# Gate and up with four paired slabs in a row: the residual kept in DRAM, its tiles used for summed weights, and a fifth weight place

## The chip, the cores and the metric

The kernel runs on one core of a Trainium2 chip. The metric is the device time of one execution in microseconds (us). The kernel computes everything in 32-bit floats; each factor of a product is split into a high part that TensorE multiplies exactly enough and a low part, and a product is made of three matmuls (high x high, high x low, low x high).

## The reference, cut to what matters

One encoder block over 256 rows of 2048 features: four mixers side by side, cross attention, and a gated MLP, each added to the residual `x`, then a last norm. The change lies in the MLP:

```python
def swiglu(h, w_gate_up, w_down):
    gate, up = jnp.split(h @ w_gate_up, 2, axis=-1)
    return (jax.nn.silu(gate) * up) @ w_down
...
        x = x + swiglu(rms_norm(x, norm_g[l, 2]), w_gate_up[l], w_down[l])
    return rms_norm(x, final_norm_g)
```

`w_gate_up` is 2048 x 11264, `w_down` is 5632 x 2048. The residual `x` isn't read between the norm ahead of `w_gate_up` and the sum behind `w_down`.

## The kernel before, in words

**Weights come as a stream.** All weights lie in DRAM as 296 slabs of 16 blocks of 128 x 128, 1 MB each, in the order of use. Class `Stream` loads a slab into one of three `raw` buffers (`_load`, L94, on the queue of SyncE, SP), and splits it in halves or phases: ScalarE (ACT) casts the piece to the high part `wh` (L135, L147), VectorE (DVE) subtracts it for the low part `wl` (L136, L148). A piece's `wh` and `wl` lie in a *place*. Three places come from the pool `wp`, a fourth from the pool `st.extra`, which takes every fourth piece (L90). `_fill` (L166) sees to it that three pieces beyond the one in use are begun, two where there is no `extra`. `take` (L177) and `take_sums` (L192) hand the pieces to TensorE (PE).

**Two kinds of slab.** In `paired_rows` (L463) a plan of letters says how each slab is used. An N slab is plain: 16 blocks, each row of four times two halves of the 256 rows, eight parts of three matmuls of 512 columns (L432 to L434), 24 matmuls. An S slab holds the blocks of two k tiles for two column blocks (gate and up) and is multiplied with the two halves of the rows as a 2 x 2 by 2 x 2 block product in seven products instead of eight, by sums of weight blocks and of activations: seven parts, 21 matmuls. Its pieces come in four phases (`_sums`, L140): two raw quarters, one raw quarter, two sums, two sums, that is 1024, 512, 1024 and 1024 columns. The sums of activations (`combine`, L437) are made once, in tiles `z`.

**Sums made by the transfer.** For S slabs of gate and up (`SUMMED`) the third phase's two sums are made by DMA: two loads of the last quarter into both halves of a tile `two` (L101, SP), and then a load of the middle quarters that adds onto it, issued by GpSimd (L102, POOL). This is requested at the load of the slab just before the S slab; there are two such tiles. `raw` then needs only three quarters (L105, 768 KB), and DVE makes two additions (L158) instead of four.

**Order of the MLP.** `gate_up` (L1047) first makes columns 0 to 511 of gate and up plainly (slabs 120 to 127, `gemm_rows`), and meanwhile the combinations of the first activations by a background generator. Then come ten groups (j = 1 to 10) of 8 slabs, each with the plan `GROUP = "NNSNSNSN"`, L45. When the last S slab of a group is through, `mixed` (L1064) adds up four of the eight PSUM banks, `gated` (L1073) makes the silu of gate, and at the group's end `upped` (L1079) multiplies and `store_turned` (L553) writes the result to DRAM. The banks of the paired sums and the others change their roles from group to group (`swap`). `fetch` (L1087) loads the results back as activations `f` of the down product and splits them: 22 of 44 during the groups, the others afterwards, since they lie in the tiles `z` and `h3` that the groups still use. `down` (L1138) makes two passes of 22 slabs with plans of their own; it adds to the residual, tiles `res`, when its sums are through. There the S slabs load the whole slab and DVE makes all four sums.

A background (class `Background`, L204) holds the generators; `poll` lets one go a step when the DVE work owed is small. The framework orders the instructions of an engine by its own priorities, the SP queue and POOL run ahead as far as buffers are free.

Of the kernel before, what the change touches and what calls it, by code (L numbers as in the profile page):

```python
# [23 lines left out]
P = 128  # L24
# [20 lines left out]
GROUP = "NNSNSNSN"  # L45
# [3 lines left out]

PAIRED = {a + i for a, plan in [(GATE_UP + 8 * j, GROUP) for j in range(10)] + [(DOWN, PASSES[0]), (DOWN + 22, PASSES[1])]  # L50
          for i, x in enumerate(plan) if x == "S"}
SUMMED = {i for i in PAIRED if i < DOWN}
# [201 lines left out]
class Block:  # L254
# [208 lines left out]
    def paired_rows(self, w, cols, slots, sums, plan, mixed, first, ready=None, late=0, before=None, swap=False):  # L463
# [23 lines left out]
        for i, kind in enumerate(plan):  # L487
            if before:
                before(i)
            if kind == "S":  # L490
# [76 lines left out]
    def run(self):  # L567
# [21 lines left out]
        self.gk = [nc.dram_tensor(f"state{i}", (R, P), F32, kind="Internal").ap() for i in range(4)]  # L589
        self.vd = nc.dram_tensor("values", (P, 8 * 512), F32, kind="Internal").ap()  # L590
# [18 lines left out]
        with self.tc.tile_pool(name="wx", bufs=1) as st.extra:  # L609
            self.attention(self.mixers())  # L610
# [256 lines left out]
    def attention(self, ps):  # L867
        tc, nc, act, st = self.tc, self.nc, self.act, self.st
        with tc.tile_pool(name="atp", bufs=1) as atp, tc.tile_pool(name="kp", bufs=1) as kp, \
# [111 lines left out]
            st.extra = None  # L981
# [65 lines left out]
    def gate_up(self, gp, f, z):  # L1047
# [77 lines left out]
        ps = self.gemm_rows("w_gate_up", [0, DFF], self.h3,  # L1125
                            parts=[(range(8), [0]), (range(8, 12), [0]), (range(12), [1]), (range(12, 16), [0]), (range(12, 16), [1])],
                            before=lambda n: n in (1, 3) and self.bg.drain(self.late if n == 1 else last))
# [3 lines left out]
        early = self.bg.add(fetch(0, FT - 22, 3, 2.0, 15))  # L1131
        self.bg.drain(comb)
        for j in range(1, DFF // 512):
            upped(j, self.paired_rows("w_gate_up", [j * 512, DFF + j * 512], self.h3, sums, GROUP, mixed, gated, swap=j % 2 == 0)[0])
        self.bg.drain(early)
        self.fetch = self.bg.add(fetch(FT - 22, FT, 6, SOON))

    def down(self, f, sp):  # L1138
# [54 lines left out]
        for i, plan in enumerate(PASSES):  # L1193
# [5 lines left out]
            def before(j):  # L1199
                while plan[j] == "S" and len(made) <= plan[:j].count("S"):  # L1200
                    self.bg.step(next(e for e in self.bg.q if e[0] is g))
                if late and j == len(plan) - 2:
                    st.extra = None
# [687 lines left out]
```

## Time and profile before

| what | us |
|---|---|
| runs shown, median of 3 | 1436.53 (1435.76 to 1437.61) |
| the profiled execution | 1434.72 |
| its span in the trace | 1432.9 |
| TensorE busy | 1423.0 |
| VectorE busy | 1145.7 |
| ScalarE busy | 815.8 |

The profiled execution's own time is 1.8 us longer than its span. Busy time of an engine is the union of its instructions. A window's line gives its length and then, engine by engine, busy time and number of instructions, the granted clock of TensorE as a share of full speed, the mean busy share of the 16 DMA engines and the GB/s that they moved. A grouped line gives busy time, mean ns of one instruction, idle time of the engine ahead of them and what ended it. Durations of neighbours on one engine overlap somewhat; the distance from start to start is the pitch. q1 is the DMA queue that SP issues on, q0 that of POOL.

### The profile page before, as it was taken

The page shows a single profiled execution, that of the slowest core. Times are in us where ns is not written, and L with a number is a line of the kernel's source. Part 1 is how long each engine was busy: PE and PEld are TensorE (multiplying, and loading weights), DVE is VectorE, ACT ScalarE, POOL GpSimd, SP SyncE. Part 2 cuts the span into 40 slices and gives each one's busy share as a digit, 9 for nine tenths or more (in the row PEclk, how much of TensorE's full clock was granted, in tenths as well). Part 3 has the DMA queues.
Part 4 walks back from the last instruction along what each step waited for, and adds up shares of the span by engine and source line. Part 5 has one row for each costly group of instructions (what it writes and reads, how often), then busy time and mean ns, then how long its engine had stood idle before and what let it go on. Part 6 is the DMA issues. An engine that isn't in the chain of part 4 may idle for free.

```text
span 1432.9 us, 18653 instructions
## 1 busy us (share of the span) xinstructions
PE 1423.0 (99%) x6589; PEld 1181.4 (82%) x6589; DVE 1145.7 (80%) x1738; ACT 815.8 (57%) x1183; POOL 234.6 (16%) x306
## 2 busy tenths in 40 slices
PE   9999999999999999999999999999999999999997
PEld 8888888888888888888888888888888888788886
DVE  6667868777877767777677888889888888989997
ACT  7556565446745555556455556555555556655655
POOL 0000100013212223531430121122011002000000
PEclk9999999999999999999999999999999999999999
DMA  9877554456667787865986989899999887665554
GB/s 350 299 291 247 205 202 166 171 172 224 198 199 232 235 271 246 275 201 171 287 242 207 283 280 289 275 275 285 294 293 289 264 265 227 217 231 180 193 219 147
DMA packets 73038, 343.80 MB, mean 240 GB/s; under 512 B 10957, under 2 KB 12654, under 8 KB 45168
## 3 DMA queue, kind: packets, MB, share of 16 engines
q1 hardware_dynamic: 54848, 288.98, 57.6%
q0 software_dynamic: 17664, 52.97, 15.6%
q8 instruction: 51, 0.84, 0.2%
q10 hardware_dynamic: 432, 0.66, 0.1%
q14 instruction: 43, 0.35, 0.1%
HBM read 322.12 MB, written 20.45 MB: 239 GB/s over the span
## 4 chain that ended last, share of the span: by engine, by line
PE 98%; DVE 1%; DMA 0%; ACT 0%; issue 0%; SPq 0%; ACTq 0%
PE pg L432 22%; PE pg L433 22%; PE pg L434 22%; PE pm L432 7%; PE pm L434 7%; PE pm L433 7%; PE pg L380 4%; PE pg L381 2%; PE pm L1344 1%; PE pm L1022 1%; PE pm L993 1%; PE pm L1753 0%; DMA raw<-in_W 0%; DVE res L282 0%; PE pm L994 0%; PE pm L1518 0%
## 5 line engine op out<-in xcount | busy, mean ns | idle before, releaser
L136 DVE TENSOR_TENSOR wl<-raw,wh 128x1024 fp32r<-128x1024 f32 (+1 forms) x413 | 494.1, 1211 | 167.6 <-ACT wh L135 164.8
L135 ACT CAST wh<-raw 128x1024 fp32r<-128x1024 f32 (+1 forms) x413 | 424.7, 1043 | 282.9 <-PE pg L434 188.3
L432 PE MATMUL pg<-wh,act 128*128 128x512 f32 (+1 forms) x1191 | 465.5, 391 | 0.0
L433 PE MATMUL pg<-wl,act 128*128 128x512 f32 (+1 forms) x1191 | 463.9, 389 | 0.1
L434 PE MATMUL pg<-wh,act 128*128 128x512 f32 (+1 forms) x1191 | 463.8, 390 | 0.0
L432 PEld LDWEIGHTS pg<-wh,act 128*128 128x128 f32 x1191 | 224.0, 188 | 47.9 <-issue 1.5
L434 PEld LDWEIGHTS pg<-wh,act 128*128 128x128 f32 x1191 | 223.9, 188 | 47.5 <-DVE act L282 0.6
L433 PEld LDWEIGHTS pg<-wl,act 128*128 128x128 f32 x1191 | 224.0, 188 | 46.5 <-DVE wl L136 1.2
L147 ACT CAST wh<-raw 128x1024 fp32r<-128x1024 f32 (+1 forms) x150 | 137.4, 921 | 149.6 <-PE pg L434 53.8
L148 DVE TENSOR_TENSOR wl<-raw,wh 128x1024 fp32r<-128x1024 f32 (+1 forms) x150 | 155.9, 1060 | 52.8 <-ACT wh L147 52.6
L433 PE MATMUL pm<-wl,act 128*128 128x512 f32 x309 | 120.3, 389 | 0.1
L432 PE MATMUL pm<-wh,act 128*128 128x512 f32 x309 | 120.2, 389 | 0.0
L434 PE MATMUL pm<-wh,act 128*128 128x512 f32 x309 | 120.2, 389 | 0.0
L380 PE MATMUL pg<-act,wh 128*128 128x512 f32 x256 | 90.5, 395 | 0.0
L381 PE MATMUL pg<-act,wl 128*128 128x256 f32 x256 | 71.8, 280 | 0.0
L433 PEld LDWEIGHTS pm<-wl,act 128*128 128x128 f32 x309 | 58.0, 188 | 12.3 <-DVE wl L136 0.4
L434 PEld LDWEIGHTS pm<-wh,act 128*128 128x128 f32 x309 | 58.0, 188 | 12.1
L432 PEld LDWEIGHTS pm<-wh,act 128*128 128x128 f32 x309 | 58.0, 188 | 12.0
L102 POOL DMA_DIRECT2D two<-in_W x30 | 26.6, 885 | 237.6 <-DMA two<-in_W 106.4
L158 DVE TENSOR_TENSOR raw<-raw 128x512 f32<-128x512 f32 x90 | 61.8, 687 | 1.2
L147 ACT CAST wh<-two 128x1024 fp32r<-128x1024 f32 x30 | 31.5, 1051 | 52.0 <-PE pg L434 27.0
L380 PEld LDWEIGHTS pg<-act,wh 128*128 128x128 f32 x256 | 48.1, 188 | 10.5
(375 smaller groups left out, 1819.3 us busy)
## 6 DMA issues: line engine op xcount, KB each, us to landing
raw<-in_W SPq DMA_DIRECT2D x216, 1024.0 KB, 5.6
raw<-in_W SPq DMA_DIRECT2D x30, 768.0 KB, 6.3
two<-in_W SPq DMA_DIRECT2D x60, 256.0 KB, 4.8
two<-in_W POOLq DMA_DIRECT2D x30, 512.0 KB, 9.0
raw<-in_W SPq DMA_DIRECT2D x11, 512.0 KB, 7.1
hidden<-g POOLq DMA_DIRECT2D x22, 256.0 KB, 3.8
tmp<-hidden POOLq DMA_DIRECT2D x44, 128.0 KB, 6.0
features<-tmp POOLq DMA_DIRECT2D x32, 128.0 KB, 5.2
```

Source lines behind the costliest of these rows:

```text
L102: nc.gpsimd.dma_start(t, W[:, 512:1536], accum_op=ALU.add)
L135: nc.scalar.copy(wh[:, a:b], r[:, a:b])
L136: nc.vector.tensor_tensor(out=wl[:, a:b], in0=r[:, a:b], in1=wh[:, a:b].bitcast(F32), op=ALU.subtract)
L147: nc.scalar.copy(wh, src)
L148: nc.vector.tensor_tensor(out=wl, in0=src, in1=wh.bitcast(F32), op=ALU.subtract)
L158: nc.vector.tensor_tensor(out=out, in0=a, in1=b, op=ALU.add)
L380: self.nc.tensor.matmul(p[:, :], wh, slot[:, :], start=start, stop=False)
L381: self.nc.tensor.matmul(p[:, 0:R], wl, slot[:, 0:R], start=False, stop=stop)
L432: self.nc.tensor.matmul(p, hi, wh, start=start, stop=False)
L433: self.nc.tensor.matmul(p, hi, wl, start=False, stop=False)
L434: self.nc.tensor.matmul(p, lo, wh, start=False, stop=stop)
L993: nc.tensor.matmul(p[:, :], q[d][:, r * P:(r + 1) * P], kt[d][:, :], start=d == 0, stop=False)
```

## The change

- **Plan.** `GROUPS` holds one plan, `"NNSSSSNN"`, for all ten groups: four S slabs in a row between two N slabs on each side, where there were three S slabs alternating with N. A fourth combination of activations is needed: `z` has four tiles instead of three and `f` has 12 tiles of its own instead of 14. The order in which S slabs use the `z` tiles is turned by one.
- **Residual outside.** When the first gemm of gate and up is two slabs on (`before(1)`), the four `res` tiles, 128 x 1024 each, are written to DRAM on SP's queue. After the tenth group they are loaded back on the same queue.
- **Summed tiles.** In between these four tiles take the place of the two tiles `two`, one after the other. `AHEAD` says at which slab the sums are requested: for the S slabs 2, 3, 4 and 5 of a group at slab 6 of the group before and at slabs 0, 1 and 3.
- **Fifth place.** The pool `tw` of the two tiles goes; a pool `wz` gives a fifth place from `before(1)` on until slab 5 of group 10. `ring` lists the pools; a piece goes to the one used longest ago, and `_fill` keeps as many pieces ahead as there are further places, four instead of three.
- **Fetch.** 20 activations are fetched during the groups and 24 afterwards.

```diff
-GROUP = "NNSNSNSN"
+GROUPS = "NNSSSSNN",
...
+AHEAD = {2: -2, 3: 0, 4: 1, 5: 3},
+
+SUMS = {GATE_UP + 8 * j + a: GATE_UP + 8 * j + i for j in range(10) for i, a in AHEAD[j % len(GROUPS)].items()}
+
+SUMMED = {GATE_UP + 8 * j + i for j in range(10) for i, x in enumerate(GROUPS[j % len(GROUPS)]) if x == "S"}
...
-        self.extra = self.sums = None
+        self.ring = [[self.wp, -1] for _ in range(3)]
+        self.sums = []
...
-        pool = self.extra if self.extra and len(self.halves) % 4 == 3 else self.wp
+        slot = min(self.ring, key=lambda x: x[1])
+        assert slot[1] < self.at or slot[1] < 0
+        pool, slot[1] = slot[0], len(self.halves)
...
-        if n // 16 + 1 in SUMMED:
-            W, t = self.W[n // 16 + 1], self.sums.tile([P, 1024], F32, name="two", tag="two")
+        if n // 16 in SUMS:
+            W, t = self.W[SUMS[n // 16]], self.sums[0]
+            self.sums.append(self.sums.pop(0))
             for a in (0, 512):
                 nc.sync.dma_start(t[:, a:a + 512], W[:, 1536:2048])
             nc.gpsimd.dma_start(t, W[:, 512:1536], accum_op=ALU.add)
...
-        ahead = self.at + 1 + min(3 if self.extra else 2, self.n // 16)
+        ahead = self.at + 1 + min(len(self.ring) - 1, self.n // 16)
         while len(self.halves) < ahead and self.made < NBLK:
             self._half()
+
+    def lend(self, pool):
+        self.ring.append([pool, -1])
+        return pool
+
+    def back(self, pool):
+        self.ring = [x for x in self.ring if x[0] is not pool]
...
+        self.rd = nc.dram_tensor("residual", (P, 4 * 1024), F32, kind="Internal").ap()
...
-            f = [fp.tile([P, 512], F32R, name=f"f{i}") for i in range(14)]
-            z = [fp.tile([P, 1024], F32R, name=f"z{i}") for i in range(3)]
-            f = act[4:12] + f + [z[i // 2][:, i % 2 * 512:i % 2 * 512 + 512] for i in range(6)] + self.h3
-            with tc.tile_pool(name="wy", bufs=1) as self.st.extra:
-                self.gap(self.st.extra, 64)
-                with tc.tile_pool(name="tw", bufs=2) as self.st.sums, tc.tile_pool(name="gp", bufs=1) as gp:
+            f = [fp.tile([P, 512], F32R, name=f"f{i}") for i in range(12)]
+            z = [fp.tile([P, 1024], F32R, name=f"z{i}") for i in range(4)]
+            f = act[4:12] + f + [z[i // 2][:, i % 2 * 512:i % 2 * 512 + 512] for i in range(8)] + self.h3
+            with tc.tile_pool(name="wy", bufs=1) as self.wy:
+                self.gap(self.wy, 64)
+                self.st.lend(self.wy)
+                with tc.tile_pool(name="wz", bufs=1) as self.wz, tc.tile_pool(name="gp", bufs=1) as gp:
                     self.gate_up(gp, f, z)
...
-        sums = [((2 * i, 2 * i + 1), z[i]) for i in range(GROUP.count("S"))]
+        sums = [((2 * i, 2 * i + 1), z[(i + 1) % 4]) for i in range(4)]
         comb = self.bg.add(combined())
+        whole = [x.rearrange("p k r -> p (k r)") for x in self.res]
+
+        def before(n):
+            if n == 1:
+                self.st.lend(self.wz)
+                for c, x in enumerate(whole):
+                    nc.sync.dma_start(self.rd[:, c * 1024:(c + 1) * 1024], x)
+                self.st.sums = list(whole)
+            if n in (1, 3):
+                self.bg.drain(self.late if n == 1 else last)
...
-        early = self.bg.add(fetch(0, FT - 22, 3, 2.0, 15))
+        early = self.bg.add(fetch(0, FT - 24, 3, 2.0, 15))
         self.bg.drain(comb)
         for j in range(1, DFF // 512):
-            upped(j, self.paired_rows("w_gate_up", [j * 512, DFF + j * 512], self.h3, sums, GROUP, mixed, gated, swap=j % 2 == 0)[0])
+            plan = GROUPS[(j - 1) % len(GROUPS)]
+            upped(j, self.paired_rows("w_gate_up", [j * 512, DFF + j * 512], self.h3, sums[:8 - plan.count("N")], plan, mixed, gated,
+                                      before=lambda i: (j, i) == (10, 5) and self.st.back(self.wz), swap=j % 2 == 0)[0])
+        for c, x in enumerate(whole):
+            nc.sync.dma_start(x, self.rd[:, c * 1024:(c + 1) * 1024])
         self.bg.drain(early)
-        self.fetch = self.bg.add(fetch(FT - 22, FT, 6, SOON))
+        self.fetch = self.bg.add(fetch(FT - 24, FT, 6, SOON))
```

More of the change, by code (lines that the diff above doesn't have):

```diff
@@ L489, in paired_rows @@
                 before(i)
-            if kind == "S":
+            if kind in "Ss":
                 ks, z = next(todo)
@@ L608, in run @@
         nc.scalar.copy(self.identr, self.ident)
-        with self.tc.tile_pool(name="wx", bufs=1) as st.extra:
+        with self.tc.tile_pool(name="wx", bufs=1) as self.wx:
+            st.lend(self.wx)
             self.attention(self.mixers())
@@ L980, in attention @@
             late.append(self.bg.add(self.arrive(self.xf[1], 2, self.tmp, self.put3, FAR), go=True))
-            st.extra = None
+            st.back(self.wx)
             self.add_rows(1, 3, self.gemm_rows("w_xo", [1536], o)[0])
@@ L1121, in combined @@
                 yield from self.combine(z, *(self.h3[k] for k in ks))
-        sums = [((2 * i, 2 * i + 1), z[i]) for i in range(GROUP.count("S"))]
+        sums = [((2 * i, 2 * i + 1), z[(i + 1) % 4]) for i in range(4)]
         comb = self.bg.add(combined())
+        whole = [x.rearrange("p k r -> p (k r)") for x in self.res]
[7 more added lines that the diff above has]
+                self.bg.drain(self.late if n == 1 else last)
         ps = self.gemm_rows("w_gate_up", [0, DFF], self.h3,
                             parts=[(range(8), [0]), (range(8, 12), [0]), (range(12), [1]), (range(12, 16), [0]), (range(12, 16), [1])],
-                            before=lambda n: n in (1, 3) and self.bg.drain(self.late if n == 1 else last))
+                            before=before)
         self.bg.drain(col)
@@ L1202, in before @@
                 if late and j == len(plan) - 2:
-                    st.extra = None
+                    st.back(self.wy)
             ps, rest = self.paired_rows("w_down", [2 * i * 512, (2 * i + 1) * 512], f, sums[:n], plan,
```

5 lines of the change are left out of this document (2 added, 3 removed).

## The prediction

> **What bounds the kernel now.** I read the page first, then the stretch of the gate and up product in windows, grouped lines, DMA and waits, and last the order of time on single engines.
>
> ```profile
> span 1432.9 us, 18653 instructions
> PE 1423.0 (99%) x6589; PEld 1181.4 (82%) x6589; DVE 1145.7 (80%) x1738; ACT 815.8 (57%) x1183; POOL 234.6 (16%) x306
> ...
> PE 98%; DVE 1%; DMA 0%; ACT 0%; issue 0%; SPq 0%; ACTq 0%
> ```
>
> TensorE (PE) is busy for 99% of the span and is 98% of the chain that ended last. So only fewer or faster matmuls shorten this kernel, and everything else costs nothing until PE has to wait for it. The change touches the ten groups of gate and up. Their length is read from the copy that ends the paired sums, which comes once in each group:
>
> ```profile
> L1067 ACT COPY g<-pm x5: 579/579/579, 810.4 to 1142.3; 128x512 f32<-128x512 f32 x5
> ```
>
> From 810.4 to 1142.3 are eight groups (every second one ends on the other set of banks), so a group takes 331.9 / 8 = 41.49 us. It holds five N slabs of 24 matmuls and three S slabs of 21, together 183, so PE starts one every 41.49 / 183 = 0.2267 us. An N slab is 5.44 us of PE, an S slab 4.76. Windows of one group each show what the others do (first and last of eight; DVE lies between 35.20 and 36.88, mean 36.2):
>
> ```profile
> core 0: us, PE busy (x) PEld busy (x) DVE busy (x) ACT busy (x) POOL busy (x), PEclk, DMA share, GB/s
> 738.70:776.00 37.30, 37.30 (x166) 30.87 (x165) 26.40 (x56) 21.37 (x31) 4.12 (x5) 1.00 0.69 216
> ...
> 817.50:859.00 41.50, 41.50 (x185) 34.32 (x184) 36.38 (x45) 23.95 (x29) 7.60 (x9) 1.00 0.91 280
> ...
> 1108.00:1149.50 41.50, 41.50 (x184) 34.36 (x183) 35.20 (x41) 22.87 (x25) 4.21 (x5) 1.00 0.90 272
> ...
> 1191.00:1220.00 29.00, 29.00 (x129) 24.03 (x128) 27.07 (x43) 17.80 (x28) 10.34 (x12) 1.00 0.83 239
> 1220.00:1260.00 40.00, 39.93 (x174) 31.99 (x173) 38.32 (x70) 23.98 (x41) 2.64 (x3) 1.00 0.63 234
> ```
>
> PE never pauses, at granted clock 1.00. But DVE is at 36.2 of 41.5 us and the DMA engines at 0.90 to 0.94: two suppliers stand close behind PE, and the change asks more of both.
>
> **The matmuls.** One N slab of each group becomes an S slab: one part of three matmuls less. Ten groups times 3 times 0.2267 us = **-6.8 us**, all on the path. A group's floor becomes 180 x 0.2267 = 40.81 us.
>
> **DVE and ACT.** The grouped lines of the same eight groups:
>
> ```profile
> L136 DVE TENSOR_TENSOR wl<-raw,wh 128x1024 fp32r<-128x1024 f32 x80 | 94.6, 1216 | 6.5 <-ACT wh L135 5.6
> ...
> L148 DVE TENSOR_TENSOR wl<-raw,wh 128x1024 fp32r<-128x1024 f32 x48 | 58.6, 1222 | 32.2 <-ACT wh L147 32.1
> L147 ACT CAST wh<-raw 128x1024 fp32r<-128x1024 f32 x48 | 50.3, 1047 | 52.9 <-DVE raw L158 15.9 <-PE pg L434 10.6 <-PE pm L434 10.3
> ...
> L158 DVE TENSOR_TENSOR raw<-raw 128x512 f32<-128x512 f32 x24 | 16.5, 689 | 0.6
> L148 DVE TENSOR_TENSOR wl<-raw,wh 128x512 fp32r<-128x512 f32 x24 | 16.4, 683 | 0.0
> L158 DVE TENSOR_TENSOR raw<-two,raw 128x512 f32<-128x512 f32 x24 | 16.4, 682 | 0.0
> L147 ACT CAST wh<-raw 128x512 fp32r<-128x512 f32 x24 | 14.9, 620 | 13.1 <-PE pg L434 7.6 <-PE pm L434 5.4
> ```
>
> An N slab takes two subtractions of 1.22 us. An S slab takes three of them (raw, summed tile, raw again), one of 0.68 and two additions of 0.68 and 0.69. Back to back they overlap a little, as the order of time on DVE shows: two take 2.28 us from start to start (1009.17 to 1011.45), and 512 columns after 1024 leave 0.6.
>
> ```profile
> 1009.17 2.36 DVE L136 TENSOR_TENSOR wl<-raw,wh 128x1024 fp32r<-128x1024 f32 x2
> 1011.45 0.42 DVE L282 TENSOR_TENSOR f<-tmp,f 128x256 fp32r<-128x256 f32 x1
> ...
> 1037.52 0.68 DVE L158 TENSOR_TENSOR raw<-raw 128x512 f32<-128x512 f32 x1
> 1039.69 1.23 DVE L148 TENSOR_TENSOR wl<-raw,wh 128x1024 fp32r<-128x1024 f32 x1 [1.49 <-ACT wh L147]
> ```
>
> So by pitch an N slab is 2.28 us of DVE and an S slab 3 x 1.14 + 0.60 + 2 x 0.66 = 5.34. The exchange adds 3.06 us per group: 36.2 + 3.1 = 39.3 of 40.81 us, 96%. ACT gets 3.77 instead of 2.09 us, in all some 25.5 of 40.8, which is free. Can DVE be that full without holding PE? The second pass of the down product says yes:
>
> ```profile
> 1296.00:1316.00 20.00, 20.00 (x90) 16.54 (x90) 20.00 (x33) 11.16 (x18) 0.00 (x0) 1.00 0.60 211
> 1316.00:1336.00 20.00, 20.00 (x90) 16.58 (x89) 19.98 (x29) 12.37 (x16) 0.00 (x0) 1.00 0.56 210
> ```
>
> For 40 us DVE has no idle time there and PE no pause. But S and N alternate there; four S in a row need 21.4 us of DVE in 19.0 us of PE, and the fifth place must carry that. By hand, with time zero at the group's start: two N slabs end at 10.88, S slabs at 15.6, 20.4, 25.2 and 29.9. With five places the first phase of the second S gets its place at 10.88; its cast takes 1.05 and a handshake, so DVE starts it at about 12.1. Three S slabs by pitch end at 28.1; PE wants the third and the last phase of the fourth S at 27.2 and 28.6, when DVE has them at 27.0 and 28.1. The slack of 0.2 to 0.5 us is eaten by the chain inside a slab, second addition, cast, last subtraction:
>
> ```profile
> 1038.60 1.05 ACT L147 CAST wh<-raw 128x1024 fp32r<-128x1024 f32 x1 [2.26 <-DVE raw L158]
> ```
>
> The addition ended at 1038.20 and the cast began at 1038.60; 0.40 + 1.05 us after the addition against 1.14 of the subtraction of the summed tile, which can lie between: 0.3 to 0.4 us idle per slab, or 1.5 where that subtraction came earlier, as here. The low end of what PE loses is nothing (the full 40 us above), the high end three waits of 0.9 us (35.6 us in 39 waits, the row below) less the slack, 2.3 us per group. The row nearest to a dense row of S slabs is that of the full DVE, so I take a little above its zero: 0.25 us per group, **+2.5 us**.
>
> ```profile
> DVE wl L148 <- ACT wh L147: 35.6, 39, 1.6
> ...
> ACT wh L135 <- DMA raw<-in_W: 28.8, 9, 4.2
> ```
>
> **DMA.** The same eight groups (332 us):
>
> ```profile
> q1 hardware_dynamic: 16168, 73.65, 63.4%
> q0 software_dynamic: 6032, 20.32, 28.4%
> ...
> raw<-in_W SPq DMA_DIRECT2D x41, 1024.0 KB, 7.0
> raw<-in_W SPq DMA_DIRECT2D x24, 768.0 KB, 6.3
> two<-in_W SPq DMA_DIRECT2D x48, 256.0 KB, 4.7
> two<-in_W POOLq DMA_DIRECT2D x24, 512.0 KB, 9.6
> ```
>
> A group takes 26.3 us of all 16 engines on q1 (2.86 us per MB) and 11.8 on q0 (4.64 per MB), 38.1 together. An S slab loads 768 KB and twice 256 KB on q1 and accumulates 512 KB on q0, in place of one load of 1024 KB: 0.26 MB and 0.52 MB more, 0.75 + 2.43 = 3.2 us. At today's price that is 41.3 us, above PE's floor. Loads that stand behind each other without pause go cheaper:
>
> ```profile
> 1270.00:1274.00 4.00, 4.00 (x19) 3.34 (x18) 3.96 (x10) 2.38 (x5) 0.00 (x0) 1.00 1.01 412
> ```
>
> 412 GB/s at a full share are 2.43 us per MB; with that on q1 the group needs 9.47 x 2.43 + 14.2 = 37.2 us. I take the middle, 39.3, so no price by itself; both ends stay in the range. The sums' own lateness goes: they are requested two to four slabs ahead instead of one, against 4.7 + 9.6 us to land, and four tiles in turn are free long before their next use, so SP and POOL have nothing to stand behind there.
>
> The Trainium skill says in "DMA: Bandwidth & Descriptors", section "Issuing engines are not separate DMA queues", that transfers started by sync, scalar or gpsimd end on the same 16 engines and interleave. By that rule the fourth accumulate is not free beside the loads, and a group could not go below the engines' sum, which is the DMA rival below. The trace agrees in so far as q1 and q0 add up to the windows' share (63.4 and 28.4% against 0.90 to 0.94).
>
> **The moves.** The residual's way out and back is 2.1 MB each, 6 us of all engines at 2.86 per MB. Out, it lies in the first gemm, whose share of 0.69 leaves 11 us of 37; SP's weight loads queue behind, with three raw buffers and up to five places as cover. Back, it stands on SP ahead of the third slab's load of the down product; 0.83 and then 0.63 leave 5 and 15 us. Both nothing; without the cover up to 6 us each. The fourth combination of activations, about 2.8 us of DVE, lies in that first gemm, DVE 26.40 of 37.30: nothing. The paired sums now have two N slabs (10.9 us) to leave their banks instead of one: nothing, or a gain nobody waits for. The last activations: 24 instead of 22 tiles are fetched late, and the first is needed two tiles (2.7 us) sooner.
>
> ```profile
> 1203.43 0.76 DVE L282 TENSOR_TENSOR z<-tmp,z 128x256 fp32r<-128x256 f32 x2
> ```
> ```profile
> 1206.40 0.39 PE L432 MATMUL pg<-wh,z 128*128 128x512 f32 x1
> ```
>
> The first is ready at about 1203.85 and used at 1206.40, 2.5 us of slack. The split may move up as far, but into the end of the last group's sums: between 0 and 3 us, I take **+0.5**.
>
> **The sum.** -6.8 + 2.5 + 0.5 = -3.8 us. The profiled execution took 1434.72 us, 1.8 around its span, and becomes 1430.9; the median of the runs is 1436.53, 1.8 above it, so I carry the difference over: **1432.7 us**. That case's own range is 1429.7 (all 6.8) to 1433.6. About 0.2%, 2.9 us, is what a measurement of this kernel can tell from no change.
>
> **The rivals.** *DMA sets the pace* at 41.3 us per group: 10 x (41.3 - 41.49) = -1.9, 1434.6, with the late tiles 1435: no change to be told. For it speak the shares, and nine waits of ACT for raw weights (28.8 us, up to 4.2) that occur already; against it, that backlogged loads go at 2.43 per MB. *The row of four starves PE*: the cast chain costs DVE its 0.9 us wait in each slab, and PE loses 1.0 to 2.3 us at the end of the row, less the 0.68 won: +0.3 to +1.6 per group, 1440 to 1453, the lower half likelier, since not every slab waits so long: 1444. It decides from 0.7 us lost per group on. For it: 21.4 us into 19.0, with 0.2 to 0.5 us of slack; DVE's total with four such waits, 39.3 + 3.6, is over the floor too. Against it: most of today's waits end with a place that PE frees, and the fifth place thins those. A raw load late behind two sums in the same stretch lands in the same place and adds to it. *The fifth place brings no lead*, since cast chain and raw loads set the pace: that is the same loss at its upper end.
>
> **How the numbers follow.** Forecast 0.42; DMA pace, or a gain eaten by the row, 0.20; starved row 0.38 (a fifth of it above 1449). The range to leave out a tenth above and little below: 1429.5 to 1449. Faster 0.42, same 0.20, slower 0.38.
>
> **What would show it.** Right: 30 matmuls fewer, groups of 41.0 to 41.2 us, DVE at 39 to 40 per group, PE's waits below 0.4 us a group. Wrong: PE waiting for wl of L148 or wh of L147 at the fourth S; DMA share at 1.0 and long waits for raw (DMA); a pause near the first z or f tiles of the down product (late tiles). A group longer than 41.5 us in most of the ten would make the forecast's sign wrong.

## The result, and the profile after

The changed kernel takes **1491.26 us** (median of 4 runs, 1486.2 to 1494.8), the kernel before beside it 1436.14: a ratio of 1.038, interval 1.0343 to 1.0417. It is slower by 3.8%, and above the range that was given. The page of its profiled execution (1486.2 us):

```profile
span 1484.1 us, 18676 instructions
PE 1439.3 (97%) x6559; PEld 1173.6 (79%) x6559; DVE 1176.1 (79%) x1786; ACT 825.9 (56%) x1205; POOL 243.0 (16%) x316
...
PE 21%; DVE 13%; DMA 8%; issue 7%; ACT 3%; POOL 0%; SPq 0%; ACTq 0%; DVEq 0%; POOLq 0%
```

The 30 matmuls are gone (6559 for 6589), the span is 51.2 us longer, and PE, 98% of the last chain before, is 21% of it now; VectorE (DVE) and DMA have come in. The copy that ends the paired sums gives a group's length, as before:

```profile
L1085 ACT COPY g<-pm x5: 581/587/587, 810.7 to 1170.5; 128x512 f32<-128x512 f32 x5
```

(1170.5 - 810.7) / 8 = 44.98 us on average over eight groups, against 41.49. Matmuls can be counted off in order of time, which cuts both executions into the same stages:

| stage (us) | before | after | more |
|---|---|---|---|
| start of the first gemm of gate and up | 734.42 | 738.67 | 4.25 |
| that gemm | 43.52 | 46.71 | 3.19 |
| group 1 | 41.48 | 41.23 | -0.25 |
| groups 2 to 9, mean (floor now 40.81) | 41.49 | 44.67 | 8 x 3.18 |
| group 10 | 41.48 | 56.00 | 14.52 |
| down product to the last matmul | 231.18 | 235.91 | 4.73 |

Three things happen, each with its own lines.

**The start: SP's queue stands behind the residual.** What SP issues around it (its timeline, then its waits from 700 to 750 us, then the same of the other engines from 725 to 745):

```profile
709.74 0.33 SPq L116 DMA_DIRECT2D raw<-in_W  x1
714.45 0.33 SPq L1149 DMA_DIRECT2D residual<-res  x1
723.59 0.33 SPq L109 DMA_DIRECT2D res<-in_W  x1
724.02 0.37 SPq L116 DMA_DIRECT2D raw<-in_W  x1
```
```profile
SPq L109 <- DMA residual<-res: 10.5, 2, 8.4
```
```profile
ACT wh L143 <- DMA raw<-in_W: 9.1, 1, 9.1
```

L109 loads weight sums into a tile of the residual, so it waits until that tile has been written out, 8.4 us in one piece. SP takes its instructions in order, so the plain weight load of L116 behind it goes out 14.3 us after the one before (the first 4.7 of them are the time until the residual's own write goes out), and the cast of those weights (L143) waits 9.1 us.

**The groups.** Waits in the stretch that the prediction used (817 to 1149 us, eight groups before and 7.4 of the longer ones now), then DMA there:

```profile
ACT wh L143 <- DMA raw<-in_W: 54.5, 16, 6.0
ACT wh L155 <- DVE raw L166: 52.4, 17, 5.6
```
```profile
raw<-in_W SPq DMA_DIRECT2D x28, 1024.0 KB, 9.9
raw<-in_W SPq DMA_DIRECT2D x31, 768.0 KB, 4.8
...
tmp<-hidden POOLq DMA_DIRECT2D x8, 128.0 KB, 6.0
```

The cast of N weights waits 54.5 us for raw loads (28.8 before), and a load of 1024 KB lands after 9.9 us instead of 7.0. The cast of S weights waits 52.4 us for the additions (15.9 before). Here is DVE in one row of four S slabs:

```profile
1058.65 1.78 DVE L156 TENSOR_TENSOR wl<-raw,wh 128x1024 fp32r<-128x1024 f32 x2
1060.35 0.68 DVE L166 TENSOR_TENSOR raw<-res,raw 128x512 f32<-128x512 f32 x1
1060.95 1.22 DVE L156 TENSOR_TENSOR wl<-res,wh 128x1024 fp32r<-128x1024 f32 x1
1062.09 0.68 DVE L166 TENSOR_TENSOR raw<-raw 128x512 f32<-128x512 f32 x1
1063.96 2.96 DVE L156 TENSOR_TENSOR wl<-raw,wh 128x1024 fp32r<-128x1024 f32 x3 [1.19 <-ACT wh L155]
...
1080.36 1.23 DVE L144 TENSOR_TENSOR wl<-raw,wh 128x1024 fp32r<-128x1024 f32 x1 [0.60 <-ACT wh L143]
```

From 1058.65 to 1080.36 are 21.7 us of DVE for 19.0 us of PE. In every S slab of this row the subtraction of the summed tile (`wl<-res`) lies *between* the two additions, 1.74 us from the one to the other. The last cast needs the second addition; in the first slab DVE has nothing else then and idles 1.19 us, in the other three it goes on with pieces of the next slab. Counted off slab by slab over groups 2 to 9, 3.2 of the 3.9 us that a group loses to its floor go in the four S slabs, 1.67 in the second and 0.87 in the fourth.

**The end of the groups.** PE's longest wait is for the first activation `f` of the down product; POOL then loads twelve pieces of the hidden activations in a row:

```profile
PE pg L447 <- ACT f L305: 10.9, 1, 10.9
```
```profile
1233.90 1.49 POOL L574 DMA_DIRECT2D hidden<-g  x2 [39.05 <-DVE g L572]
1235.38 10.52 POOL L579 DMA_DIRECT2D tmp<-hidden  x12
```

In the stretch above only 8 such loads were made (its last row), and no more between 820 and 1180 us; before there were 27:

```profile
tmp<-hidden POOLq DMA_DIRECT2D x27, 128.0 KB, 5.9
```

And TensorE comes back from the pause at half its clock (windows):

```profile
1225.00:1230.00 5.00, 4.13 (x19) 3.08 (x17) 3.32 (x4) 5.00 (x9) 0.00 (x0) 1.00 0.79 293
1235.00:1240.00 5.00, 0.01 (x1) 0.02 (x1) 4.03 (x11) 0.40 (x1) 5.00 (x7) 0.50 0.83 197
1240.00:1245.00 5.00, 5.00 (x12) 3.94 (x13) 1.67 (x4) 1.21 (x3) 5.00 (x6) 0.50 0.99 284
1245.00:1250.00 5.00, 5.00 (x22) 4.06 (x21) 2.42 (x4) 3.34 (x7) 4.52 (x7) 0.92 1.05 145
```

### The profile page after: what moved, and what is told of

Read it like the earlier page. It is cut to its first block, busy times and chain, and to the rows that moved or that the text cites. A ratio compares the mean times of both kernels' runs of the same rounds, so it can differ in the third digit from the quotient of the medians.

```text
span 1484.1 us, 18676 instructions
## 1 busy us (share of the span) xinstructions
PE 1439.3 (97%) x6559; PEld 1173.6 (79%) x6559; DVE 1176.1 (79%) x1786; ACT 825.9 (56%) x1205; POOL 243.0 (16%) x316
## 4 chain that ended last, share of the span: by engine, by line
PE 21%; DVE 13%; DMA 8%; issue 7%; ACT 3%; POOL 0%; SPq 0%; ACTq 0%; DVEq 0%; POOLq 0%
DMA raw<-in_W 8%; DVE wl L156 5%; PE pg L448 4%; PE pg L449 4%; PE pg L447 4%; DVE wl L144 3%; PE pm L448 3%; PE pm L449 3%; PE pm L447 3%; DVE raw L166 2%; ACT wh L155 1%; ACT wh L143 1%; DVE h L297 1%; DVE h L301 1%; DMA ar<-features 1%
## 5 line engine op out<-in xcount | busy, mean ns | idle before, releaser
L143 ACT CAST wh<-raw 128x1024 fp32r<-128x1024 f32 (+1 forms) x393 | 404.1, 1041 | 328.9 <-PE pg L449 182.1
L447 PE MATMUL pg<-wh,act 128*128 128x512 f32 (+1 forms) x1166 | 456.9, 393 | 5.4 <-ACT wh L143 5.4
L448 PE MATMUL pg<-wl,act 128*128 128x512 f32 (+1 forms) x1166 | 456.5, 392 | 1.9 <-DVE wl L144 1.7
L449 PE MATMUL pg<-wh,act 128*128 128x512 f32 (+1 forms) x1166 | 455.4, 391 | 0.4 <-DVE act L297 0.4
L447 PEld LDWEIGHTS pg<-wh,act 128*128 128x128 f32 x1166 | 219.8, 189 | 54.1 <-ACT wh L143 7.0
L449 PEld LDWEIGHTS pg<-wh,act 128*128 128x128 f32 x1166 | 219.6, 188 | 46.9 <-DVE act L297 1.3
L448 PE MATMUL pm<-wl,act 128*128 128x512 f32 x284 | 111.7, 393 | 1.8 <-DVE wl L144 1.7
L447 PE MATMUL pm<-wh,act 128*128 128x512 f32 x284 | 110.5, 392 | 0.9 <-ACT wh L143 0.9
L449 PE MATMUL pm<-wh,act 128*128 128x512 f32 x284 | 110.4, 390 | 0.0
L110 POOL DMA_DIRECT2D res<-in_W x40 | 35.2, 881 | 242.6 <-DVE wl L156 91.7
L166 DVE TENSOR_TENSOR raw<-raw 128x512 f32<-128x512 f32 x100 | 68.6, 686 | 0.6
L447 PEld LDWEIGHTS pm<-wh,act 128*128 128x128 f32 x284 | 53.2, 188 | 13.3 <-ACT wh L143 2.2
L449 PEld LDWEIGHTS pm<-wh,act 128*128 128x128 f32 x284 | 53.4, 188 | 10.8
L448 PE MATMUL pg<-wl,z 128*128 128x512 f32 x112 | 45.2, 403 | 5.7 <-DVE wl L156 5.7
```

The source lines that it names most:

```text
L143: nc.scalar.copy(wh[:, a:b], r[:, a:b])
L166: nc.vector.tensor_tensor(out=out, in0=a, in1=b, op=ALU.add)
L447: self.nc.tensor.matmul(p, hi, wh, start=start, stop=False)
L448: self.nc.tensor.matmul(p, hi, wl, start=False, stop=False)
L449: self.nc.tensor.matmul(p, lo, wh, start=False, stop=stop)
```

## The experiments

All of them beside the kernel before. "Groups" is the mean of groups 2 to 9, first matmul to first matmul (before 41.49, floor of the new plan 40.81).

| run | groups | us | ratio | interval |
|---|---|---|---|---|
| the change | 44.67 | 1491.26 | 1.038 | 1.0343 to 1.0417 |
| e1_sums_in_place | 45.27 | 1486.3 | 1.0344 | 1.0306 to 1.0382 |
| e2_fetch_stepped | 46.37 | 1484.89 | 1.0334 | 1.0289 to 1.038 |
| e3_row_alone | 50.27 | 1535.51 | 1.0687 | 1.0637 to 1.0737 |
| e4_plan_back | 42.71 | 1455.07 | 1.0127 | 1.0089 to 1.0164 |
| e5_spread | 43.67 | 1482.57 | 1.0319 | 1.0248 to 1.039 |
| e6_no_accumulate | 42.78 | 1463.14 | 1.0184 | 1.0154 to 1.0213 |
| e7_fourth_raw | 44.90 | 1482.21 | 1.0316 | 1.0286 to 1.0346 |
| e8_no_additions | 41.64 | 1439.16 | 1.0027 | 1.0008 to 1.0045 |
| e9_store_first | 44.61 | 1477.51 | 1.029 | 1.0245 to 1.0334 |
| e10_store_first_no_accumulate | 42.50 | 1459.08 | 1.0161 | 1.0126 to 1.0196 |
| e11_fourth_raw_fifth_place | 42.25 | 1459.61 | 1.0165 | 1.0135 to 1.0194 |
| e12_plan_back_in_place | 42.71 | 1451.36 | 1.011 | 1.0083 to 1.0137 |
| e13_mended | 42.84 | 1449.6 | 1.0108 | 1.0076 to 1.014 |
| e14_mended_order | 41.38 | 1438.41 | 1.0013 | 1.0002 to 1.0023 |
| e15_plan_back_order | 41.72 | 1439.52 | 1.0016 | 1.0004 to 1.0029 |
| e16_order | 43.22 | 1468.44 | 1.0227 | 1.0214 to 1.024 |
| e17_pairs | 41.23 | 1434.65 | 0.9988 | 0.9976 to 1.0 |
| e18_pairs_fetch | 41.31 | 1433.7 | 0.9984 | 0.9969 to 0.9998 |

**One part at a time.** e1 ties the sums' loads to the place where the program issues them, so that they can't move ahead of plain loads on SP's queue:

```diff
+            mark = len(nc.cur_bb.bb.instructions)
             for a in (0, 512):
                 nc.sync.dma_start(t[:, a:a + 512], W[:, 1536:2048])
+            self.keep_place(mark)
```

> The loads of the sums keep their place on SP's queue in the order of the program (slab 6 of the group before, slabs 0, 1 and 3), where the changed kernel's queue has all four of them in the row of S slabs, each as soon as its tile is free and ahead of the plain slabs' loads. Order theory (plain loads stand behind the sums): issue to landing of 1024 KB loads back from 9.8 to about 7 us, groups 2 to 9 from 44.7 to 41.0-42.0 us, and the 4.3 us pause ahead of the first gemm of gate and up gone, since the residual's writes no longer hold loads up there; in all 25 to 35 us less than 1486. Row theory (DVE cannot feed four S slabs in a row): groups stay at 44 or more, PE still waits at the row's end. Total theory (the 16 DMA engines are full): groups stay at 44 or more with a DMA share of 0.95 or more.

The late start falls from 4.25 to 0.81 us and the first gemm's loss from 3.19 to 1.63. The groups gain nothing (45.27): the order on SP explains the start only. And the 1024 KB loads land after 6.2 us now, sooner than in the kernel before (7.0), while the casts wait no less for them than the 54.5 us of the change (817 to 1149 us), so their time to landing isn't what the groups lose:

```profile
raw<-in_W SPq DMA_DIRECT2D x28, 1024.0 KB, 6.2
```
```profile
ACT wh L145 <- DMA raw<-in_W: 62.0, 18, 6.1
```

e2 lets the fetch go a step at four slabs of each group:

```diff
+            e = [e for e in self.bg.q if e[0] is early]
+            if e and i in (0, 1, 6, 7):
+                self.bg.step(e[0])
```

> The early fetch of the down product's activations gets a step by hand at each N slab of the ten groups, instead of waiting until the DVE work owed is small; all else as changed. Starved-fetch theory (the bookkeeping of owed DVE work never falls below its bound in the new groups, so 12 loads and 11 splits are left for the end): the 11.3 us pause ahead of the down product goes and with it the lower clock behind it, 13 to 16 us less; groups 2 to 9 as before at 44 to 45.5. Rival (the first late tile is late whatever is done early, since its load stands behind the last store of the hidden layer): the pause keeps 6 us or more.

Now 27 fetch loads lie between 820 and 1180 us, and the pause of 11.25 us is gone (group 10: 43.10). But the other groups grow by 1.7 us, the start is later still (741.37 us), and most of what was won is lost. e3 is the row of four without the rest: two tiles `two` of its own, four places, sums one slab ahead, the residual stays. e4 is the old plan with all the rest:

```diff
-GROUPS = "NNSSSSNN",
+GROUPS = "NNSNSNSN",
-AHEAD = {2: -2, 3: 0, 4: 1, 5: 3},
+AHEAD = {2: 0, 4: 2, 6: 4},
```

> The plan with four S slabs in a row alone: two sum tiles of their own, requested one slab ahead, four places, the residual stays in its tiles. Row theory: groups at least as long as 44.7, rather longer (46 to 49), since a place is missing. Order theory: with two tiles only two sums can be asked for early, the plain loads stand behind fewer of them, but sums come late; 43 to 46. Residual theory for the pause ahead of the first gemm (a sum's load waits on SP for the residual's write): the pause of 4.3 us and the 3.2 us in the first gemm go.

> Residual outside, four sum tiles and the fifth place as changed, but the plan NNSNSNSN of before, sums asked for two slabs ahead. Row theory: groups at 41.5, as before the change; only the start keeps its 7 us. Order theory: groups of 41.5 to 43, as sums still go ahead of plain loads, but one less per group. Total theory: 41.5 with a DMA share of 0.92. Starved-fetch theory: DVE work owed falls below its bound again, so no pause ahead of the down product.

The row alone costs 8.8 us a group, so the tiles and the fifth place do help; its start (734.26 us) and its first gemm (43.52) are those of the kernel before, so the loss there goes with the residual's way out. And even under the old plan the rest costs 1.2 us a group, where nothing should. e5 spreads the S slabs on top of e1 (`"NSNSNSSN"`):

> Four S slabs in each group as changed, but spread: plan NSNSNSSN, the sums' loads in the program's place (the run with the sums in place is the one to compare, groups 2 to 9 mean 45.3 us). Bunching theory (N slabs in a row free the raw buffers every 2.3 us of DVE, so four plain loads and three pairs of sums are asked for at once and land 10 to 14 us later, then the row of S slabs runs without a lead): groups of 41.0 to 42.5. Total theory (DMA engines or DVE are too full for four S slabs in any order): groups stay at 44 or more.

Groups of 43.67, a pause of 8.3 us in the first one and one ahead of the down product; the total is no better. The first pause comes from the fetch: on ACT the cast of a fetched activation stands ahead of the next cast of N weights, and waits for its load (785 to 810 us):

```profile
ACT act L317 <- DMA tmp<-hidden: 12.5, 1, 12.5
```

That load went out late, after POOL had been idle for 14.1 us; why, the trace doesn't show.

**Transfers or DVE?** On e1, e6 leaves out the accumulating load, e8 the additions, and e7 makes the fifth place a fourth raw buffer:

```diff
-            nc.gpsimd.dma_start(t, W[:, 512:1536], accum_op=ALU.add)
```
```diff
-                ops = ((s[1], t[:, 0:512], s[2]), (s[2], s[1], s[0]))
+                ops = ()
```
```diff
-                self.st.lend(self.wz)
+                self.st.rawx = self.wz
```

> Sums in place, and the accumulating loads left out (the summed tiles hold the last quarter alone, so the product is not the reference's): 0.52 MB less per S slab on q0, all engine work as it was. If transfers hold up the raw loads (bunching or total theory), 1024 KB and 768 KB loads land in 5 to 6 us and groups go to 41.0 to 42.0. If DVE cannot feed the row of four (row theory), groups stay at 44 or more.

> Sums in place; the memory of the fifth place holds a fourth raw buffer instead, so four places as before. Buffer theory (a raw load can only be asked for when one of three buffers is free, and that round trip sets the pace): groups 41.5 to 43. Place theory (the row of four lives from the fifth place): 45 to 48, since the lead inside the row is gone.

> Sums in place; the two additions of each S slab on DVE left out (so the last phase is not the reference's), 1.3 us of DVE less per S slab, 5.3 per group, transfers as they were. Row theory: DVE needs 4.0 us per S slab in 4.76 of PE, groups 40.8 to 41.5. Total theory of the DMA: 43 to 44.5, as the engines' work is the same; bunching theory in between, 42 to 43.5, since a raw buffer is held 1.3 us less.

Without the accumulate the groups are 2.5 us shorter (42.78), without the additions 3.6 (41.64, group 10 at 40.80). With a fourth raw buffer but four places each group takes 44.9. e8 also bears on the rival that DMA sets the pace. Its window of 270 us (DMA share and GB/s stand last):

```profile
870.00:1140.00 270.00, 266.00 (x1164) 217.91 (x1164) 222.77 (x254) 164.14 (x192) 51.49 (x60) 1.00 0.98 297
```

All loads are made there, at a share of 0.98, and PE starts 1164 matmuls in 270 us, 0.232 us each against 0.2267 at the floor. That speaks against the rival; e17 below decides it. Late loads alone don't make the loss either: between 817 and 1149 us e8 waits longer for them than e1 does, but its DVE has 5.3 us less to do in each group and makes it good.

```profile
ACT wh L145 <- DMA raw<-in_W: 67.2, 23, 5.1
```

e9 and e10 test whether the epilogue of a group, in order on ACT and DVE ahead of the next N slab, is the cause: the next group's second N slab is begun behind it.

```diff
-        ahead = self.at + 1 + min(len(self.ring) - 1, self.n // 16)
+        ahead = self.at + 1 + min(len(self.ring) - 1 - self.hold, self.n // 16)
...
+            self.st.hold = 2 if i == 7 and j < 10 else 0
```

> Sums in place, and at the last slab of each group the pieces of the next group's second N slab are begun two steps later in the program, behind the group's last sums, the store of the hidden layer and so on, instead of ahead of them. In-order theory (DVE's epilogue of a group stands behind the subtractions of an N slab whose load is 10 to 14 us late, and so the row of S slabs starts 3 to 5 us late on DVE): groups 2 to 9 from 45.3 to 42.0-43.5 us. Rival (the row of four itself is too long for DVE whenever it starts, or the late load is needed by PE as soon): groups stay at 44.5 or more.

> The same, and the accumulating loads left out (the summed tiles hold the last quarter alone, so the product is not the reference's). In-order theory: with the loads on time the order of the epilogue matters little; groups 41.0 to 42.5, against 42.7 without the new order. Row theory: 42.5 to 43, what DVE needs for the row of four.

Groups of 44.61 and 42.50, that is 0.66 less than e1 and 0.28 less than e6: e9 misses what the theory asked for, e10 lies where its range and the rival's meet and doesn't decide. The epilogue's order is a small part at most. e11 finds room for both a fourth raw buffer and the fifth place, by giving up one of four arrival tiles (`ar`); e13 adds e2's fetch at slabs 0, 6 and 7. e12 is e4 with e1's order on SP.

> Sums in place, five places, and a fourth raw buffer in memory of its own (one small arrival tile comes from another pool for that). Buffer theory (three raw buffers make the plain loads late, a late load makes the row late): groups 41.0 to 42.5, and no wait for raw over 2 us in the groups. Row theory: 43 to 44.5, between this and the steady 44.85 that four raw buffers gave with four places. Total theory of the DMA fell with the run without additions, whose groups reach 40.8 at a DMA share of 0.98.

> Plan NNSNSNSN of before with residual outside, four sum tiles, fifth place, and the sums' loads in the program's place. If the row of four is what costs in the groups and the order of the sums is what cost 1.2 us a group in the run with only the plan put back: groups at 41.5, no pause ahead of the first gemm, in all within 5 us of before. If the tiles in DRAM or the fifth place cost by themselves: groups stay near 42.7 and the total near 1455.

> All that the runs showed to help, with the plan of four S slabs: sums in place, five places, a fourth raw buffer, and the early fetch stepped by hand three times per group. If the pause ahead of the down product comes only from the starved fetch: it goes (13 to 16 us less than 1459.6), and groups grow by what the splits ask of a full DVE, 0.9 to 1.5 us each: 1452 to 1458. If DVE had room in the groups: 1443 to 1447. Faster than before would need groups of 41.1 or less, which no run with all of the work has had.

The fourth buffer takes 3.0 us off the groups (45.27 to 42.25) where it does not cost a place. e13 has no pause ahead of the down product either (group 10: 41.29) and is at 1449.6. But e13 with its new plan and e12 with the old one both stay at 42.7 to 42.8: something that the two share was still unnamed. The waits of e12, over the stretch from 817 to 1149 us, pointed to it:

```profile
ACT wh L157 <- DVE raw L168: 84.6, 23, 5.7
```

That wait of the casts for the additions was 15.9 us before.

**The order on DVE.** In e12 and e13, as in the changed kernel, the summed tile's subtraction lies between the two additions of every S slab between 1000 and 1042 us. In the kernel before, two of the three slabs between 1000 and 1042 us have their additions 0.7 us apart. Counted over groups 2 to 9, the subtraction lies between them in 8 of 24 S slabs before, in 27 of 32 in the changed kernel and in e13, and in all 24 of e12. e14 (on e13), e15 (on e12) and e16 (on e1) tie that subtraction behind the second addition and change nothing else:

```diff
+        if ph == 2 and summed:
+            self.behind(sub, self.second)
...
-                nc.vector.tensor_tensor(out=out, in0=a, in1=b, op=ALU.add)
+                self.second = nc.vector.tensor_tensor(out=out, in0=a, in1=b, op=ALU.add).ins
```

> The kernel with a fourth raw buffer, the fifth place and the stepped fetch (groups of 42.84 us), with one thing more: on VectorE the subtraction of the summed tile must follow the second of the two additions of its slab. Until now it stood between them in every S slab, so the two additions began 1.73 us apart instead of 0.7, and the cast of the last two sums waited for the second. If this order is what is left of the loss in the row of four: up to 1.0 us per S slab, groups of 41.0 to 41.6, in all 1432 to 1438. If VectorE's amount of work in the row is the loss, whatever its order, or raw loads landing late: groups of 42.5 to 43.0, 1447 to 1451.

> The plan of before with all else as changed and the sums' loads in place (groups of 42.71 us), with the same order on VectorE. In the kernel before most S slabs have their two additions next to each other, here none had. Theory of the order: groups back to 41.5 to 41.9, in all 1437 to 1443. Theory that something else of the change (the residual's tiles, the places in turn) makes the groups longer: 42.4 to 43, 1449 to 1453.

> The change with the sums' loads in place (groups of 45.27 us, 1486) and this order alone, with three raw buffers. Theory of the order: it takes its part of the 4.5 us over the floor, some 1.4 us, and leaves the late raw loads: groups of 43.5 to 44.3, 1467 to 1478. If the loads alone set the pace in this kernel: 45.0 to 45.4, 1484 to 1487.

All three go the way of the order: 42.84 to 41.38, 42.71 to 41.72, 45.27 to 43.22. DVE in e14 (L161 is the subtraction, L173 the addition):

```profile
1004.14 0.68 DVE L173 TENSOR_TENSOR raw<-res,raw 128x512 f32<-128x512 f32 x1
1004.86 0.69 DVE L173 TENSOR_TENSOR raw<-raw 128x512 f32<-128x512 f32 x1
1005.46 1.22 DVE L161 TENSOR_TENSOR wl<-res,wh 128x1024 fp32r<-128x1024 f32 x1
1006.74 2.96 DVE L161 TENSOR_TENSOR wl<-raw,wh 128x1024 fp32r<-128x1024 f32 x3
```

The additions are 0.72 us apart, and the subtraction of the summed tile covers the last cast: the work follows itself without idle time. What the order saves stands in DVE's own wait for the casts of S weights, in e1 and then in e16 (817 to 1149 us):

```profile
DVE wl L158 <- ACT wh L157: 15.3, 16, 1.2
```
```profile
DVE wl L158 <- ACT wh L157: 0.3, 1, 0.3
```

In e1 that wait is 2.1 us for each of the 7.3 groups, as much as the groups of e16 gain. The casts' wait for the additions, which pointed here, is no such measure: it is 45.1 us in e1 and 67.4 in e16, where ACT has time to spare. The fourth raw buffer is worth something beside it: the waits of N casts for raw loads in e16 (three buffers) and in e14 (four), over the same stretch:

```profile
ACT wh L145 <- DMA raw<-in_W: 57.0, 19, 5.9
```
```profile
ACT wh L148 <- DMA raw<-in_W: 27.1, 13, 5.1
```

e17 keeps all that e14 has and splits the row in two pairs; e18 moves the fetch to slabs at which no sums are requested:

```diff
-GROUPS = "NNSSSSNN",
+GROUPS = "NNSSNSSN",
-AHEAD = {2: -2, 3: 0, 4: 1, 5: 3},
+AHEAD = {2: 0, 3: 1, 5: 3, 6: 4},
...
-            if e and i in (0, 6, 7):
+            if e and i in (0, 4, 7):
```

> The mended kernel with the order on VectorE (1438.4 us; groups of 41.38, and a pause of 3.4 us in the first gemm, where the residual's way out, the first sums and the arrivals meet), with its four S slabs in two pairs, NNSSNSSN, the sums requested at slabs 0, 1, 3 and 4 of their own group and the fetch stepped at slabs 0, 4 and 7. If the row of four is what still holds the groups above 40.81, two pairs give 40.8 to 41.1; if requests that no longer fall into the first gemm end its pause, that is 2 to 4 us less: 1431 to 1435 in all. If the DMA engines, at a share of 0.99 in the groups, are the bound now, groups stay at 41.3 to 41.6 and the total at 1435 to 1440.

> The kernel with two pairs of S slabs (1434.65 us, eight of ten groups at 40.8, one at 43.6, where a raw load issued behind four fetch loads and an accumulate took 13.7 us to land), with the fetch stepped at slabs 2, 6 and 7, at which no sums are requested, instead of 0, 4 and 7. If fetch loads that meet the sums' loads are what makes single groups long: ten groups at 40.8 to 41.0, 1430 to 1433. If such a late load comes by chance of the traffic or the fetch's work on VectorE now meets the S slabs: groups of 41.2 or more, 1434 to 1438.

In e17 seven of ten groups take 40.8 us, the floor, one 41.0, one 41.3 and one 43.6. That settles the DMA rival: it had named 41.3 us per group, and e14 with its 41.38 fits that at a share of 0.99 between 776 and 980 us, but e17 makes the same loads there, and most of its groups take 40.80. In the chain of the long group stands a raw load of 13.7 us:

```profile
1010.97 13.72 DMA raw<-in_W
```

e18 has other single groups above the floor (41.6, 42.5, 42.4), so such a load is not the fetch's doing alone; where each comes from stays open. e17 is at 0.9988 and e18 at **0.9984** of the kernel before (0.9969 to 0.9998): the lowest medians of all, e18 by 0.16%, less than the 0.2% that counts here as a difference.

## Why the prediction was wrong, step by step

**The matmuls** were right: 30 fewer and a floor of 40.81, which e17 and e18 reach in single groups (40.80). Over the ten groups e17 keeps 3.4 of the 6.8 us.

**The row of four**, costed at 0.25 us per group, is the step that failed most. The groups lie 3.86 us above the floor, 44.67 against 40.81. On e1, at 45.27, the runs take it apart: the order on DVE 2.05 (e16), the fourth raw buffer another 1.84 (to e14, stepped fetch included), and 0.57 left (from 41.38 to the floor). Of this rest 0.55 is lost in the fourth S slab, where the prediction's working by hand had its slack of 0.2 to 0.5 us, and seven of the ten groups of e17, with two pairs, are without it. The shares depend on which comes first: ahead of the order, the fourth buffer takes off 3.02 (e1 to e11), and the order behind it 1.46 (e13 to e14).

The prediction had both first parts in its hands. It saw an early subtraction of the summed tile cost 1.49 us of idle time in one slab, and then took the row "nearest to a dense row of S slabs", the full DVE of the down product. There all sums are made by DVE and nothing waits for a summed tile, so that row could not show the case. It also said that a late raw load "lands in the same place and adds to it", and added nothing for it.

What the change itself did was to make the early subtraction the rule. That this order costs what it costs is shown by three runs; why the framework chose it stays open. The earlier request alone isn't the reason: e3 requests the sums one slab ahead, as the kernel before, and has the subtraction between the additions in 24 of 32 S slabs, in 15 of them with sums that landed less than 1 us ahead of their cast. One of these in e3:

```profile
851.49 0.69 DVE L165 TENSOR_TENSOR raw<-two,raw 128x512 f32<-128x512 f32 x1 [1.40 <-issue]
852.63 1.23 DVE L155 TENSOR_TENSOR wl<-two,wh 128x1024 fp32r<-128x1024 f32 x1 [0.45 <-ACT wh L154]
853.77 0.69 DVE L165 TENSOR_TENSOR raw<-raw 128x512 f32<-128x512 f32 x1
```

The work that it counted for DVE was right, and so was that DVE can be so full without holding PE: this is one group of e17 at the floor, DVE at 39.39 of 40.80 us (39.3 predicted).

```profile
1068.40:1109.20 40.80, 40.80 (x182) 33.80 (x181) 39.39 (x48) 25.08 (x29) 7.74 (x9) 1.00 0.97 308
```

The second rival, the starved row, came nearest. It had the cast chain's waits, at 1.0 to 2.3 us lost per group, and the order's 2.05 lies within that; the late raw loads, which it named without a price, make up most of the rest.

**DMA** "no price by itself" holds for the rate: the middle of the two prices, 39.3 of 40.81 us, is a share of 0.96, and e17, nearly at the floor, has just that between 776 and 980 us:

```profile
776.00:980.00 204.00, 203.83 (x899) 168.39 (x898) 189.15 (x224) 122.58 (x144) 43.07 (x50) 1.00 0.96 299
```

What it left out is the wait for a buffer. A plain load goes out when DVE has made the last subtraction from a raw buffer (in e1 SP waits 94.6 us, in 19 pieces, for that behind S slabs), and the casts then wait for the load, 54.5 us instead of 28.8. The time to landing, 9.9 us of a 1024 KB load instead of 7.0, isn't the cause, since e1 brings it to 6.2 and gains nothing in the groups; a fourth raw buffer takes 3.0 us off each.

**"SP and POOL have nothing to stand behind there"** and the residual's way out at nothing: wrong. The step looked at the four tiles in turn and not at the first use of each, which waits for the write of the residual. It cost 4.25 us ahead of the first gemm; with 3.19 in that gemm it makes 7.4, of which e1 leaves 2.4. The cover named, three raw buffers and up to five places, was gone after 14.3 us without a load. The way back was free, as said: e17 loads it from 1160 to 1182 us, inside group 10, and that group takes 40.80.

**The late tiles**, +0.5: wrong, by another way than the one examined. The tiles that are ready late were not the bound; the fetch during the groups had not been done (8 loads instead of 27). The background goes on only when little DVE work is owed, and the new groups left it no such moment: that is argued from the program, and e8 agrees with it (without the additions 24 loads are made between 817 and 1149 us), while e2 and e13 show that stepping the fetch ends the pause. The price is the 11.25 us, and 13 matmuls at 0.43 us instead of 0.23 behind it, 2.6 more. Of the down product's 4.73 some 2.1 remain in e17 and e18, which have no such pause. In e17 two starts of matmuls are 0.90 us apart at 1228.0 and two 1.34 at 1230.9, where before has nothing over 0.42 in that stretch. The first waits for DVE's split of a late tile, which is the step as it was meant, some 0.7 us; the second waits for a cast whose place PE had freed only 0.06 us earlier. Why it is later there than before stays open.

**Together**: 4.25 + 3.19 at the start, 28.5 in the groups (-0.25 + 8 x 3.18 + 3.27), 11.25 of pause, 4.73 behind it: 51.9 us for the forecast -3.8. The fourth combination and ACT's added work were free, as said: e3 makes the combination in a first gemm as long as before's, and e17 has ACT's work with most groups at the floor.

## What to carry to other kernels

On an engine that is nearly full, the order in which it is given its work is part of the price: ask of every instruction between two others who waits for the second of them. A long list of waits isn't yet a loss, so look for the engine that cannot make them good. Where a stage is to run at a supplier's limit, take its price from a row with the same chain of dependences and not from one with the same busy share. And when a background only works in gaps, closing the gaps moves its work to the first place where somebody must wait for it.

## What the runs showed of the hardware

The granted clock falls with PE's pauses. After 11.25 us without a matmul it was 0.50, and it stayed there for some 5.7 us of matmuls (1240.0 to 1245.7), one every 0.43 us instead of 0.23. A wait of 4.1 us ahead of the first gemm was followed by a window of 0.80, with 35 matmuls in 10 us instead of 44:

```profile
740.00:750.00 10.00, 9.88 (x35) 8.03 (x36) 9.56 (x18) 6.50 (x10) 2.86 (x4) 0.80 0.91 284
```

The Trainium skill, "TensorE: Matmul & The Clock Gate", section "Part 1: The HAM clock gate", gives half rate after at least one idle window of about 3.4 us, and full rate after at least one busy window of about that length. Both pauses here are longer than that and both lowered the clock, so the traces agree with the first half; the way back took 5.7 us behind the pause of 11.25, longer than one such window. A pause of PE is dearer than its length: here 11.25 us cost 13.9, with 13 matmuls at half rate.

The 16 DMA engines carried 299 GB/s at a share of 0.96 beside a TensorE close to its floor (e17, 776 to 980 us). The mean share did not tell whether a kernel is bound by them: the changed kernel itself ran at 0.89 between 780 and 1200 us and waited for loads (54.5 us between 817 and 1149).

```profile
780.00:1200.00 420.00, 402.71 (x1709) 315.56 (x1707) 353.97 (x412) 222.30 (x254) 57.81 (x68) 1.00 0.89 271
```
